# The residual of the last out-projection, scaled at other places of a hand-written order

## The chip, the cores and the metric

The kernel runs on one core of one Trainium2 chip. The metric is device time in microseconds (us), the median of 3 runs. One further execution was taken by the hardware profiler; all rows of the profile and the trace come from that one.

## What is computed

A decoder trunk of two layers on x of 512 rows (tokens) and 2048 columns, all in float32. Layer 0 is a differential attention, layer 1 a forgetting attention with 16 heads of 128 columns. Each layer ends alike:

```
y = o @ w_out                                  # out-projection, 2048 x 2048
x = layer_norm(DN_ALPHA * x + gate * y, ln_g[l], ln_b[l])
```

The change concerns layer 1. Its x is the normalised output of layer 0, x = n * g0 + b0, where the kernel keeps the plain n in DRAM and applies layer 0's weights g0, b0 (`ln_g[0]`, `ln_b[0]`) and the factor ALPHA only when the residual is needed. So the residual is ALPHA * (n * g0 + b0), and the row to be normalised is that plus gate * y.

## The kernel before

**Weights.** All products are made in three passes from two parts of each operand (`products`, L188 to L190: high x high, high x low, low x high). A `WeightStream` brings the weights of all jobs through four stage buffers (`wst`, L48, on the queue of SyncE, SP). ScalarE (ACT) rounds a stage to its high part `whi` (L108), VectorE (DVE) subtracts it to get the low part `wlo` (L109). `get` keeps this two slices ahead of the matmuls; there are three buffers of each part.

**The last out-projection** (`out_projection(oB, 1, ...)`) has four jobs, f = 0 to 3, of 512 output columns each. A job has eight slices of two 128-row weight tiles; for each slice `group` runs four bursts, one for each block b of 128 tokens, of six matmuls each. So a job has 32 bursts and 192 matmuls; each block accumulates in a PSUM bank of its own (`acc`, four in all), and job f + 1 needs the banks of job f back. In the last slice each block is evacuated by DVE: `ztmp` = acc * gate (L988), z = residual + ztmp (L1433), statistics (L990). In the last job, six of the slices are held back and run block by block, and the norm follows each block (`norm_b`).

**Pieces.** After each burst `tick` takes one entry off the list `pieces`: None, a function, or a list of functions. So other work is written between the bursts by hand. `last_pairs` puts the attention of heads 12 to 15 on that list in 50 steps (`score`, `turn`, `send`, `take`, `values`, and `og`, the split of a head's output, L184). The two half jobs ahead of the out-projection (16 bursts each) use 32 of them; 18 are left for job 0, and are steps 0 to 17 below:

```
[tc_[2]], [sd[2], tc_[3], og[8]], [rd[0], vc[0]], [vc[1], rd[1]], [sd[3], og[9]], [dd[0], dd[1], rd[2]], [og[10]],
[rd[3], dd[2]], [dd[3], og[11]], [td[0]], [td[1], og[12]], [td[2]], [td[3], og[13]], [vd[0]], [vd[1]], [], [og[14]], [og[15]],
```

Here c and d stand for heads 14 and 15. `score` is three matmuls into `sc`, the masked maximum on DVE (L1289), the exponential on ACT (L1292) and the normalisation; `turn` a transpose on DVE (L1303) and a store to DRAM (L1305); `send` four loads from there into `pTl` (L1313); `take` a cast to `pTh` on ACT (L1319) and a subtraction on DVE (L1320); `values` the matmuls into `o` and, in its second half, the head's output `ogB` on DVE (L1336).

**The residual.** `prepare(k)` calls `residual_b(f, banks)`: it issues the loads of g0, b0 (both broadcast over the partitions, L950) and of four blocks `nr` of n (L1415), and puts four functions `scaled(b)` on the list. Each is a pair on DVE, `nr = nr * ALPHA * g0` (L1419) and `nr = b0 * ALPHA + nr` (L1420), 512 columns wide. `prepare(0)` runs ahead of job 0, and looks for free (None) steps from the third on; there is one, step 15. So the four `scaled` of f = 0 stand at steps 15, 18, 19 and 20, `prepare(1)` at 21, and the `scaled` of f = 1 at 23, 25, 27 and 29. Only 28 steps can be taken ahead of job 0's first evacuation: there `drain()` runs all that is left. In job 1 `prepare(2)` stands behind eight free steps and its `scaled` at every second step after it (10, 12, 14, 16); job 2 is the same with `prepare(3)`.

**Who orders the instructions.** The order in which the code traces instructions is a priority, not the order in a queue. A planner at compile time fills each engine's queue: by its own estimates of durations and landings it takes, whenever an engine is free, the earliest traced instruction that is ready. Each engine then works through its queue in that fixed order. `tc.keep_in_program_order` (on L1419) ties an instruction behind the one that was traced last before it on the same engine; L1420 needs L1419's result. The loads have no such tie.

**Buffers.** The residual's tiles, `gate`, the heads' keys and outputs and some held weights share one pool of 16 buffers of 128 x 512 (`kpool`, tag "K"), which are given out in turn.

Of the kernel before, what the change touches and what calls it, by code (L numbers as in the profile page):

```python
# [124 lines left out]
def tile_yoco(  # L125
# [173 lines left out]
    pieces = []  # L299
# [571 lines left out]
    def drain():  # L871
        while pieces:
            tick(0)
# [71 lines left out]
    def ktile(name):  # L945
        return kpool.tile([P, T], F32, name=name, tag="K")


    def row_bcast(t, src):
        nc.sync.dma_start(t, src.partition_broadcast(P))  # L950
# [10 lines left out]
    def out_projection(jobs, layer, zp, opened, residual, norm, after_held=None):  # L961


        ready = {}

        def prepare(k):
            if k < len(jobs):
                ready[k] = residual(jobs[k][0], jobs[k][2])

        prepare(0)  # L970
        for k, (f, job, banks) in enumerate(jobs):
            if layer == 1:

                pieces.extend([None] * (8 if k else 0) + [lambda k=k: prepare(k + 1)])
            elif k:
                prepare(k)
            res = ready[k]
            gate = ktile("gate")
            row_bcast(gate, gate_dram[layer][0, 512 * f : 512 * (f + 1)])

            def evac(b, acc, f=f, res=res, gate=gate):
                if f == 0 and b == 0:
                    drain()
                    opened()
                pool, z, stats = zp
                zs = z[:, b, 512 * f : 512 * (f + 1)]
                tmp = pool.tile([P, 512], F32, name="ztmp", tag="htmp", bufs=2)
                V.tensor_tensor(tmp, acc, gate, op=ALU.mult)  # L988
                res(b, zs, tmp)
                V.bn_stats(stats[:, b, f, :], zs)  # L990
                if f == 3:
                    norm(b)

            last = k == len(jobs) - 1
            group(job, True, evac, banks, bg=1 if k == 0 and layer == 0 else 0, hold=(5, 6)[layer] if last else 0, after_held=after_held if last else None)
# [79 lines left out]
    pieces.append(lambda: split_og((14, 15)))  # L1075
    pieces.append(lambda: ab.update(kv=fold(0, ktile("mrow"))))
    out_projection(oA, 0, zp, open_n, residual_a, norm_a, lambda b, k: build_next() if b == 3 and k < 2 else None)
    npool, n, nstats = zp

# [320 lines left out]
    def open_z():  # L1400
# [3 lines left out]
        for k, src in (("g", ln_g), ("b", ln_b)):  # L1404
            lnrow[k] = pool.tile([P, D], F32, name="ln_" + k)
            row_bcast(lnrow[k], src[1, :])

    def residual_b(f, banks):
        fs = slice(512 * f, 512 * (f + 1))
        g0, b0 = ktile("g0"), ktile("b0")  # L1410
        row_bcast(g0, ln_g[0, fs])
        row_bcast(b0, ln_b[0, fs])
        nr = {b: ktile("nr") for b in banks}
        for b in banks:
            nc.sync.dma_start(nr[b], n_dram[b * P : (b + 1) * P, fs])  # L1415

        def scaled(b):

            tc.keep_in_program_order(V.scalar_tensor_tensor(nr[b], nr[b], ALPHA, g0, op0=ALU.mult, op1=ALU.mult))  # L1419
            V.scalar_tensor_tensor(nr[b], b0, ALPHA, nr[b], op0=ALU.mult, op1=ALU.add)  # L1420

        if f == 0:

            free = [k for k, piece in enumerate(pieces) if piece is None and k > 1]
            for k, b in zip(free, banks):
                pieces[k] = lambda b=b: scaled(b)
            pieces.extend(lambda b=b: scaled(b) for b in banks[len(free):])
        else:
            for b in banks:
                pieces.extend([None, lambda b=b: scaled(b)])  # L1430

        def fn(b, dst, tmp):
            V.tensor_tensor(dst, nr[b], tmp, op=ALU.add)  # L1433
        return fn

    def norm_b(b):
# [16 lines left out]
        for f0, f1 in zip((0, *ends), ends):  # L1453
            fs = slice(f0, f1)
            V.scalar_tensor_tensor(z[:, b, fs], z[:, b, fs], rstd, lnrow["b"][:, fs], op0=ALU.mult, op1=ALU.add)
            nc.sync.dma_start(out[b * P : (b + 1) * P, fs], z[:, b, fs])

    out_projection(oB, 1, zp2, open_z, residual_b, norm_b)
    drain()

# [27 lines left out]
```

## Time and profile before

| | us |
|---|---|
| median of 3 runs | 1970.49 (1969.86 to 1970.54) |
| the profiled execution | 1971.12 |
| its span, first to last instruction | 1969.3 |
| last out-projection: first matmul | 1769.30 |
| last statistics of its last block | 1958.61 |

A row of a timeline reads: start and length in us, engine, line of the kernel, operation, output <- inputs, shape, count, and in brackets the idle time before it and who ended it. PE is TensorE's matmul, PEld its weight load (which overlaps PE), DVE is VectorE, ACT ScalarE, SPq the queue of SyncE that issues the loads. A matmul's row is longer than the step from one matmul to the next, because they are pipelined. Rows named x2 hold two instructions.

### The profile page before, as it was taken

The numbers are of one execution on the slowest core, as the hardware profiler recorded it, in microseconds if no ns is written. First come the engines' busy times: TensorE is split into PE (matmuls) and PEld (weight loads), VectorE is DVE, ScalarE is ACT, GpSimd is POOL, SyncE is SP. The second block draws the span as 40 slices with busy tenths as digits, with TensorE's granted clock in tenths as the row PEclk, the third lists the DMA queues.
The fourth block names the chain that finished last, engine by engine and source line by source line (L and its number), as shares of the span: only waits on it lengthen the run. The fifth ranks groups of instructions, "written<-read, shape, count | busy, mean of one in ns | idle before, by whom it ended". The sixth has DMA issues, their size and how long they took to land.

```text
span 1969.3 us, 25096 instructions
## 1 busy us (share of the span) xinstructions
PE 1930.4 (98%) x8869; PEld 1600.0 (81%) x8869; DVE 1321.1 (67%) x2328; ACT 708.9 (36%) x1233; POOL 2.2 (0%) x10
## 2 busy tenths in 40 slices
PE   5999999999999999999999999999999999999997
PEld 4888888888888888888888888888888888887885
DVE  7885678877777777553575656566566666696557
ACT  2432445333333434431273222224343433452123
POOL 0000000000000000000000000000000000000000
PEclk8999999999999999999999999999999999999999
DMA  9993465777777775253336766664355555557432
GB/s 341 359 309 108 153 195 174 247 230 233 227 239 231 227 240 168 93 169 98 125 134 218 248 235 195 227 214 129 114 151 153 152 154 154 157 150 255 147 96 97
DMA packets 303002, 371.40 MB, mean 189 GB/s; under 512 B 57462, under 2 KB 221068, under 8 KB 302108
## 3 DMA queue, kind: packets, MB, share of 16 engines
q1 hardware_dynamic: 300496, 365.57, 58.4%
q10 hardware_dynamic: 2380, 4.21, 0.6%
q8 instruction: 70, 1.15, 0.2%
q14 instruction: 56, 0.46, 0.1%
HBM read 343.27 MB, written 26.43 MB: 188 GB/s over the span
## 4 chain that ended last, share of the span: by engine, by line
PE 94%; DVE 3%; DMA 1%; SPq 1%; issue 0%; ACT 0%; DVEq 0%; ACTq 0%
PE acc L188 28%; PE acc L189 28%; PE acc L190 28%; PE sc L189 2%; PE sc L190 2%; PE sc L188 2%; PE o L188 1%; PE o L190 1%; PE o L189 1%; DMA sms<-in_w_mod_dram 1%; SPq L497 1%; PE tr L847 0%; DVE wlo L109 0%; DMA wst<-in_b_w_out_dram 0%; PE sc L1046 0%
## 5 line engine op out<-in xcount | busy, mean ns | idle before, releaser
L109 DVE TENSOR_TENSOR wlo<-wst,whi 128x1024 fp32r<-128x1024 f32 (+2 forms) x322 | 384.0, 1194 | 374.1 <-ACT whi L108 362.2
L108 ACT CAST whi<-wst 128x1024 fp32r<-128x1024 f32 (+2 forms) x322 | 331.8, 1031 | 727.0 <-PE acc L190 354.3
L188 PE MATMUL acc<-whi,hh 128*128 128x512 f32 x1232 | 483.4, 395 | 4.6 <-DVE ztmp L988 4.2
L189 PE MATMUL acc<-wlo,hh 128*128 128x512 f32 x1232 | 481.3, 391 | 0.8 <-DVE wlo L109 0.8
L190 PE MATMUL acc<-whi,hl 128*128 128x512 f32 x1232 | 481.1, 391 | 0.0
L188 PE MATMUL acc<-hh,whi 128*128 128x512 f32 x1184 | 463.7, 392 | 0.0
L189 PE MATMUL acc<-hl,whi 128*128 128x512 f32 x1184 | 461.7, 390 | 0.0
L190 PE MATMUL acc<-hh,wlo 128*128 128x512 f32 x1184 | 461.4, 390 | 0.0
L188 PEld LDWEIGHTS acc<-whi,hh 128*128 128x128 f32 x1232 | 232.3, 189 | 51.5 <-DVE ztmp L988 4.7
L190 PEld LDWEIGHTS acc<-whi,hl 128*128 128x128 f32 x1232 | 231.9, 188 | 49.2
L189 PEld LDWEIGHTS acc<-wlo,hh 128*128 128x128 f32 x1232 | 232.3, 189 | 47.0 <-DVE wlo L109 1.1
L190 PEld LDWEIGHTS acc<-hh,wlo 128*128 128x128 f32 x1184 | 222.3, 188 | 47.3
L188 PEld LDWEIGHTS acc<-hh,whi 128*128 128x128 f32 x1184 | 222.5, 188 | 42.6
L189 PEld LDWEIGHTS acc<-hl,whi 128*128 128x128 f32 x1184 | 222.6, 188 | 42.0
L416 DVE SCALAR_TENSOR_TENSOR macc<-ms,cact,macc 128x1024 f32<-128x1024 f32 (+1 forms) x180 | 197.9, 1100 | 27.9 <-DMA ms<-in_w_mod_dram 13.4
L524 DVE SCALAR_TENSOR_TENSOR sacc<-sms,cact,sacc 128x512 f32<-128x512 f32 (+1 forms) x127 | 89.5, 705 | 4.9 <-DMA sms<-in_w_mod_dram 1.3
L751 ACT ACTIVATE e<-e,mn 128x128 f32<-128x128 f32 (+3 forms) x64 | 36.0, 563 | 101.4 <-DVE mn L747 97.9
L1292 ACT ACTIVATE eb<-eb,mnb 128x128 f32<-128x128 f32 (+1 forms) x64 | 36.1, 564 | 86.2 <-DVE mnb L1289 86.1
L747 DVE CUSTOM_DVE_ANT_0 e<-sc,bias 128x128 f32<-128x128 f32 (+3 forms) x64 | 31.1, 486 | 23.1 <-PE sc L190 20.3
L416 DVE SCALAR_TENSOR_TENSOR macc<-msk,cact,macc 128x512 f32<-128x512 f32 x60 | 45.0, 749 | 1.4
L1289 DVE CUSTOM_DVE_ANT_0 eb<-sc,biasb 128x128 f32<-128x128 f32 (+1 forms) x64 | 31.1, 486 | 17.7 <-PE sc L190 16.9
L849 ACT ACTIVATE ogT<-tr,subg 128x128 f32<-128x128 f32 x64 | 20.0, 363 | 51.3 <-PE tr L847 51.3
(261 smaller groups left out, 1756.2 us busy)
## 6 DMA issues: line engine op xcount, KB each, us to landing
wst<-in_a_w_in_dram SPq DMA_DIRECT2D x240, 256.0 KB, 3.9
ms<-in_w_mod_dram SPq DMA_DIRECT2D x64, 512.0 KB, 4.5
ms<-in_kv_w_mod_dram SPq DMA_DIRECT2D x64, 512.0 KB, 4.2
wst<-in_kv_w_dram SPq DMA_DIRECT2D x64, 512.0 KB, 3.7
sms<-in_w_mod_dram SPq DMA_DIRECT2D x56, 512.0 KB, 6.8
wst<-in_b_w_in_dram SPq DMA_DIRECT2D x112, 256.0 KB, 3.0
wst<-in_a_w_out_dram SPq DMA_DIRECT2D x32, 512.0 KB, 3.7
msk<-in_w_mod_dram SPq DMA_DIRECT2D x64, 256.0 KB, 5.5
```

The source lines that it names most:

```text
L108: self.nc.scalar.copy(hi[:, :, :w], st[:, :, :w])
L109: self.nc.vector.tensor_tensor(lo[:, :, :w], st[:, :, :w], hi[:, :, :w].bitcast(F32), op=ALU.subtract)
L188: PE.matmul(dst, lhs[0], rhs[0], start=start, stop=False)
L189: PE.matmul(dst, lhs[0], rhs[1], start=False, stop=False)
L190: PE.matmul(dst, lhs[1], rhs[0], start=False, stop=stop)
L416: ins = V.scalar_tensor_tensor(acc, w, cact[:, kt : kt + 1], acc, op0=ALU.mult, op1=ALU.add)
L524: V.scalar_tensor_tensor(acc, w, sc, acc, op0=ALU.mult, op1=ALU.add)
L747: V.tensor_tensor_reduce(out=e[:, :w], in0=sc[:, :w], in1=st["bias"][:, (3 - i) * P :], scale=-1.0, scalar=3.0e38, op0=ALU.add, op1=ALU.mi ...
L751: S.activation(e[:, :w], e[:, :w], AF.Exp, bias=mn, scale=-1.0, accum_out=rs)
L849: S.activation(ogT[2 * h + e][:, i * P : (i + 1) * P], pt[:, e * P : (e + 1) * P], AF.Copy, scale=subg[:, e : e + 1])
L1289: V.tensor_tensor_reduce(out=e[:, :w], in0=sc[:, :w], in1=bias[:, :w], scale=-1.0, scalar=3.0e38, op0=ALU.add, op1=ALU.min, accum_out=mn)
L1292: S.activation(e[:, :w], e[:, :w], AF.Exp, bias=mn, scale=-1.0, accum_out=rs)
```

## The change

The `scaled` functions get other places. Those of f = 0 are added to steps 4, 7, 11 and 13 of the list, behind what stands there. Those of f = 1 are not put on the list by `residual_b` but kept in `later`, and job 1 begins its list with them, at bursts 2, 5, 8 and 11 (from 0); `prepare(2)` follows at 12 instead of 8, with its `scaled` at 14, 16, 18 and 20. `prepare(1)` now is step 18 of job 0 instead of 21. Jobs 2 and 3 keep their lists.

```diff
         for k, (f, job, banks) in enumerate(jobs):
             if layer == 1:
 
-                pieces.extend([None] * (8 if k else 0) + [lambda k=k: prepare(k + 1)])
+                if k == 1:
+                    for piece in later:
+                        pieces.extend([None, None, piece])
+                pieces.extend([None] * (8 if k > 1 else 0) + [lambda k=k: prepare(k + 1)])
             elif k:
                 prepare(k)
...
+    later = []
+
     def residual_b(f, banks):
...
         if f == 0:
 
-            free = [k for k, piece in enumerate(pieces) if piece is None and k > 1]
-            for k, b in zip(free, banks):
-                pieces[k] = lambda b=b: scaled(b)
-            pieces.extend(lambda b=b: scaled(b) for b in banks[len(free):])
+            for k, b in zip((4, 7, 11, 13), banks):
+                pieces[k] = [*pieces[k], lambda b=b: scaled(b)]
+        elif f == 1:
+            later.extend(lambda b=b: scaled(b) for b in banks)
         else:
             for b in banks:
                 pieces.extend([None, lambda b=b: scaled(b)])
```

## The prediction

> **What bounds the kernel now.** I read the page first, then the list of waits of TensorE for the last projection, then the chain of waits and the timelines around the one wait found there.
>
> ```profile
> span 1969.3 us, 25096 instructions
> PE 1930.4 (98%) x8869; PEld 1600.0 (81%) x8869; DVE 1321.1 (67%) x2328; ACT 708.9 (36%) x1233; POOL 2.2 (0%) x10
> PE 94%; DVE 3%; DMA 1%; SPq 1%; issue 0%; ACT 0%; DVEq 0%; ACTq 0%
> ```
>
> TensorE (PE) is busy 98% of the span and is 94% of the chain, so a change to VectorE (DVE) steps pays only where TensorE waits for them. In the list of waits with TensorE alone, from 1769 to 1909 us (jobs 0, 1 and 2 of the last out-projection), there is one row:
>
> ```profile
> PE acc L188 <- DVE ztmp L988: 4.2, 1, 4.2
> ```
>
> Columns: who waits for whom, total, times, longest. It is the first matmul of job 1, which waits for the accumulator that `ztmp` (L988) of job 0's first row block must empty. The chain of waits shows what DVE did meanwhile (start, length, what):
>
> ```profile
> 1815.08 0.68 DVE nr L1420
> 1815.76 0.67 DVE nr L1419 x2
> ...
> 1816.88 1.29 DVE nr L1420 x2
> 1818.17 1.20 DVE nr L1419 x2
> 1819.37 0.60 DVE nr L1420
> 1819.98 0.60 DVE nr L1419
> 1820.58 1.20 DVE nr L1420 x2
> 1821.78 0.61 DVE ztmp L988
> 1822.44 0.80 PE acc L188
> ```
>
> Eleven instructions of `scaled` (six L1420, five L1419) run back to back from 1815.08 to 1821.78, and `ztmp` stands behind them: 6.70 us, 0.61 each. They are the rest of f = 0 (one L1420 of block 1, both of block 2) and all eight of f = 1. By the code the first L1419 of f = 0 is tied behind the DVE instruction traced before it, the output of the last attention head (L1336), and the others follow it; the four steps of f = 1 are forced out by `drain()` just ahead of job 0's evacuation.
>
> The timeline of TensorE and its busy time by stretch (length, busy and count of PE, PEld, DVE, ACT, POOL, granted clock, DMA share, GB/s) price that wait:
>
> ```profile
> 1817.82 0.39 PE L190 MATMUL acc<-whi,hl 128*128 128x512 f32 x1
> 1822.44 0.80 PE L188 MATMUL acc<-whi,hh 128*128 128x512 f32 x1 [4.23 <-DVE ztmp L988]
> ...
> 1827.17 0.40 PE L190 MATMUL acc<-whi,hl 128*128 128x512 f32 x1
> ...
> 1831.95 0.39 PE L190 MATMUL acc<-whi,hl 128*128 128x512 f32 x1
> ```
> ```profile
> 1818.20:1822.40 4.20, 0.01 (x1) 0.00 (x0) 4.20 (x8) 1.04 (x1) 0.00 (x0) 0.73 0.92 330
> 1822.40:1826.80 4.40, 4.36 (x10) 3.48 (x11) 4.40 (x8) 0.00 (x0) 0.00 (x0) 0.50 0.26 88
> 1927.20:1931.00 3.80, 3.80 (x17) 3.15 (x18) 0.48 (x1) 0.44 (x1) 0.00 (x0) 1.00 0.00 0
> ```
>
> From 1827.17 to 1831.95 lie 21 matmul steps, 0.2276 us each. The matmul after 1817.82 was due at 1818.05 and came at 1822.44: 4.39 us lost. Then the granted clock is 0.50: from 1822.44 to 1827.17 lie 11 steps in 4.73 us, where 11 x 0.2276 = 2.50 would do: another 2.23 us. The wait is worth **6.62 us**, half as much again as the list of waits says.
>
> **The change part by part.** It adds and removes no instruction: 16 pairs L1419/L1420 stay 16 pairs, and so do the loads. Only their places differ.
>
> *The four pairs of f = 1* go from the end of job 0 to bursts 2, 5, 8 and 11 of job 1, each tied behind the split of weights (`wlo`) traced before it, and those are traced behind the whole evacuation of job 0. Eight of the eleven instructions leave: 8 x 0.61 = 4.9 us. That alone would let `ztmp` start at 1815.08 + 3 x 0.61 = 1816.91; the chain has 0.66 us from its start to the matmul, so TensorE could go on at 1817.57, with 0.48 us to spare before 1818.05.
>
> *The four pairs of f = 0* go into bursts 4, 7, 11 and 13 of job 0. The other three of the eleven leave too, `ztmp` can start at 1815.08 behind the same `wlo`, and the margin grows to 1818.05 - (1815.08 + 0.66) = 2.31 us. The later row blocks follow:
>
> ```profile
> 1821.70 1.28 DVE L988 TENSOR_TENSOR ztmp<-acc,gate 128x512 f32<-128x512 f32 x2
> ...
> 1828.88 1.20 DVE L109 TENSOR_TENSOR wlo<-wst,whi 128x1024 fp32r<-128x1024 f32 x1
> ...
> 1836.86 1.22 DVE L109 TENSOR_TENSOR wlo<-wst,whi 128x1024 fp32r<-128x1024 f32 x1 [4.17 <-ACT whi L108]
> ```
>
> The evacuation takes 1821.70 to 1828.88, 7.2 us, 3.6 for two blocks (two `ztmp`, two sums, two statistics), so the fourth `ztmp` ends 3.6 + 2 x 0.61 = 4.8 us after the first starts, at 1819.9; TensorE wants that bank 18 matmuls after 1818.05, at 1822.1. The whole ends at 1822.3 and the next `wlo` at 1823.5; TensorE reaches those weights 48 matmuls into job 1, at 1829.0. After that DVE idles 4.2 us ahead of each `wlo` (last row), and a pair takes 1.2, so the four pairs cost nothing in job 1. Even all four ahead of that first `wlo` would take 4.9 of its 5.5 us.
>
> Where do the pairs of f = 0 land? DVE in job 0, and the loads on the queue of SyncE (SP) with their time to landing:
>
> ```profile
> 1763.61 0.68 DVE L184 TENSOR_TENSOR hl<-ogB,hh 128x512 fp32r<-128x512 f32 x1
> ...
> 1777.80 0.69 DVE L1289 CUSTOM_DVE_ANT_0 eb<-sc,biasb 128x512 f32<-128x512 f32 x1
> ...
> 1780.10 0.71 DVE L1303 STREAM_TRANSPOSE tb<-eb 128x512 f32<-128x512 f32 x1
> 1780.73 0.65 DVE L1320 TENSOR_TENSOR pTl<-pTl,pTh 128x512 fp32r<-128x512 f32 x1
> 1782.79 1.23 DVE L109 TENSOR_TENSOR wlo<-wst,whi 128x1024 fp32r<-128x1024 f32 x1 [1.40 <-ACT whi L108]
> ...
> 1790.20 1.23 DVE L109 TENSOR_TENSOR wlo<-wst,whi 128x1024 fp32r<-128x1024 f32 x1 [3.60 <-ACT whi L108]
> ...
> 1803.55 1.15 DVE L1320 TENSOR_TENSOR pTl<-pTl,pTh 128x384 fp32r<-128x384 f32 x2
> ```
> ```profile
> 1766.96 4.77 SPq L1313 DMA_DIRECT2D pTl<-turned  x8
> ...
> 1772.72 2.03 SPq L1415 DMA_DIRECT2D nr<-n_dram  x4
> ```
> ```profile
> DMA to landing us min/median/max: 6.3/6.5/6.6
> ```
>
> Block 0's pair is now tied behind the split L184 of head 9 (1763.61), block 1's behind the transpose at 1780.10, block 2's behind the L1320 at 1803.55, block 3's behind head 13's L184. Its operands land late: the first `nr` at 1772.72 + 6.5 = 1779.2. DVE is full until 1781.4; behind that it idles 1.4 and 3.6 us (rows 1782.79 and 1790.20). If the planner puts the three early pairs there (3 x 1.2 = 3.7 us), the idle time covers them. Without that cover they push `wlo`, whose weights TensorE reaches two slices (10.9 us) later, so nothing yet is lost. Block 2's pair delays the last split before head 15's values by 1.2 us; now both are done at 1804.7:
>
> ```profile
> 1782.37 0.19 PEld L189 LDWEIGHTS o<-pTl,vbh 128*128 128x128 f32 x1
> 1807.91 0.40 PE L188 MATMUL o<-pTh,vbh 128*128 128x512 f32 x1
> ```
>
> The values start at 1807.91, 3.2 us later, so 2.0 are left.
>
> *The loads.* `prepare(1)` moves from step 21 to 18, six issues that pass weight loads on SP; `prepare(2)` moves from burst 8 of job 1 to 12, its pairs from bursts 10 to 16 to bursts 14 to 20, the same two bursts behind their loads. Six issues hold SP about 3 us (the row of four `nr` takes 2.03). Weights have room for that: their casts wait for TensorE to free a buffer, 21 times, and never for a load between 1769 and 1909:
>
> ```profile
> ACT whi L108 <- PE acc L190: 86.5, 21, 11.0
> ```
>
> I take zero, with 0 to 1 us as bounds. Behind the removed wait nothing is late next: the evacuation, the weights and the banks have the margins above, and jobs 2 and 3 follow as they are.
>
> Sum: 1971.12 us is the profiled execution (1969.3 of span and 1.8 around it); less 6.6 it gives 1964.5. The median shown is 0.6 lower, 1970.49, so the forecast is **1963.9 us**.
>
> **The rivals.** *The early pairs hold up the attention (slower).* DVE works its queue in order. Were block 0's pair written directly behind its tie (over at 1764.3), DVE would stand until 1779.2, and 1.2 us more. All that follows would be 16.1 us late; the split at 1780.73 ends at 1781.4 and TensorE loads it at 1782.37, so 1.0 us is absorbed and TensorE loses 15.1, and 2.2 for each of one or two slow clocks. Against the 6.6 gained that is 10.7 to 12.9 us on the loss side: 1981 to 1983. The change breaks even when the pair heads DVE's queue at 1779.2 + 1.2 - 1.0 + 2.2 - 6.6 = 1775.0; earlier is a loss. For it: the tie permits it and DVE is not idle there. Against it: the planner issues by its own estimate of landings, and that estimate is late, not early:
>
> ```profile
> 1778.53 0.72 ACT L1292 ACTIVATE eb<-eb,mnb 128x512 f32<-128x512 f32 x1 [1.49 <-DVE mnb L1289]
> ...
> 1779.25 0.60 ACT L1319 CAST pTh<-pTl 128x512 fp32r<-128x512 f32 x1
> ```
>
> ScalarE (ACT) sat idle 1.49 us for the exponential, though the cast behind it stands earlier in the program. So the planner took the cast's data, sent by 1771.73, as not there yet; the loads of `nr` are queued behind those sends, and their pair must follow later still than the exponential's input at 1777.80. The Trainium skill, DMA: Bandwidth & Descriptors, Anatomy of one DMA, fits about 2.0 us plus bytes over 436 GB/s for one way of issuing, 2.6 us for 256 KB as an estimate from it. By that page the first `nr` would be there near 1775.3 and break-even would move to about 1771; the trace has 6.3 to 6.6 us and decides.
>
> *A part is given back.* A pair between 1777.80 and the split at 1780.73 makes DVE wait up to 1.4 us for the landing and work 1.2, with block 1's pair too 2.4: 1.2 to 3.8 us, less the 1.0 of slack, 0.2 to 2.8 on TensorE. The slow clock may follow: 4.2 us of waiting brought it, while the two waits at the start of job 3 did not (granted 1.00 from 1927.20, above):
>
> ```profile
> PE acc L189 <- DVE wlo L109: 0.8, 1, 0.8
> PE acc L188 <- ACT whi L108: 0.4, 1, 0.4
> ```
>
> With and without 2.2 us for the clock that makes 1964.1 to 1968.9. The Trainium skill, TensorE: Matmul & The Clock Gate, What's actually happening, says that the clock halves after an idle window of about 3.4 us; by that page the upper end would be 1966.7.
>
> *It does not take.* If pairs still stood ahead of `ztmp` when bank 0 is done, nothing would change. Four instructions suffice to use up the 2.31 us; only block 2's two are tied late, behind 1803.55, and that is 11 us ahead of 1815.08. Then 1970.5.
>
> **How the numbers follow.** Forecast 0.76, part given back 0.14, slower 0.06, no effect 0.04. The forecast's own range runs from 1966.1 (only the wait of 4.39 comes back) to 1962.7 (job 3's 1.2 us go too). With half of the second case the range 1962.7 to 1967.0 holds 0.83. A measurement here tells 0.2%, 3.9 us, from no change: below 1966.5 is faster. That is the forecast and half of the second case: 0.83 faster; the other half and the last: 0.11 the same; 0.06 slower.
>
> **What would show it.** Right: no wait of TensorE for `ztmp` at the start of job 1, the granted clock 1.00 through jobs 0 to 2, `ztmp` directly behind a `wlo` about 4 us earlier against the first matmul of job 1, four pairs among job 1's first three slices of weights, and the pairs of f = 0 in DVE's idle time behind the split at 1780.73. Wrong: a wait of TensorE for `pTl` or `sc` in job 0, an L1419 whose predecessor idles for a load of `nr`, or TensorE waiting for `wlo` early in job 1.

## The result, and the profile after

| | us |
|---|---|
| before, median of 9 runs | 1970.54 (1969.53 to 1972.77) |
| after, median of 9 runs | 1963.83 (1963.06 to 1965.51) |
| ratio, 95% interval | 0.9965, 0.9954 to 0.9975 |
| span of the profiled execution | 1969.3 before, 1963.0 after |

The kernel became 6.7 us faster; 1963.9 had been forecast. The page of the kernel after:

```profile
span 1963.0 us, 25096 instructions
PE 1929.5 (98%) x8869; PEld 1600.0 (82%) x8869; DVE 1321.6 (67%) x2328; ACT 708.9 (36%) x1233; POOL 2.2 (0%) x10
PE 95%; DVE 2%; SPq 1%; DMA 1%; ACT 0%; issue 0%; DVEq 0%; ACTq 0%
```

Every engine has the same number of instructions and, within 0.9 us, the same work; only the span is shorter. In the list of waits the row for `ztmp` is gone, as is job 3's short one for `whi`; TensorE waits for nothing from 1765 to 1910. The one row that is left of the last projection:

```profile
PE acc L189 <- DVE wlo L109: 0.8, 1, 0.8
```

Busy time by stretch of the kernel after (length, PE, PEld, DVE, ACT, POOL, granted clock, DMA share, GB/s), the first two jobs' meeting in the middle row:

```profile
1769.00:1818.00 49.00, 49.00 (x227) 41.03 (x226) 30.93 (x55) 15.87 (x27) 0.00 (x0) 1.00 0.72 236
1818.00:1822.40 4.40, 4.40 (x21) 3.66 (x20) 4.40 (x8) 1.05 (x1) 0.00 (x0) 1.00 0.46 167
1822.40:1862.00 39.60, 39.60 (x177) 32.78 (x176) 23.36 (x31) 7.38 (x7) 0.00 (x0) 1.00 0.60 189
```

PE is as long as each stretch and the clock is 1.00: before, TensorE stood for 4.2 us in the middle stretch, and behind that the clock was 0.50 from 1822.40 to 1826.80. How much did this stage itself gain? The first and the last matmul into `acc` of the last projection, in the timelines of TensorE before and after:

```profile
1769.30 0.40 PE L188 MATMUL acc<-whi,hh 128*128 128x512 f32 x1
...
1956.73 0.39 PE L190 MATMUL acc<-held,hl 128*128 128x512 f32 x1
```
```profile
1770.14 0.40 PE L188 MATMUL acc<-whi,hh 128*128 128x512 f32 x1
...
1950.36 0.39 PE L190 MATMUL acc<-held,hl 128*128 128x512 f32 x1
```

187.43 us became 180.22: 7.21 us less. The prediction's wait and clock are 6.62 of that, job 3's wait for `whi` 0.4, and 0.2 are unexplained. The execution after entered the projection 0.84 us later, ahead of any moved instruction, so that the end comes 6.4 earlier.

VectorE of the kernel after, in job 0 and around the first `ztmp`. The lines have moved: `scaled` is L1424 and L1425, `ztmp` L991, the split of `pTl` L1323:

```profile
1781.58 0.65 DVE L1323 TENSOR_TENSOR pTl<-pTl,pTh 128x512 fp32r<-128x512 f32 x1
1783.63 1.23 DVE L109 TENSOR_TENSOR wlo<-wst,whi 128x1024 fp32r<-128x1024 f32 x1 [1.40 <-ACT whi L108]
1784.77 0.69 DVE L1424 SCALAR_TENSOR_TENSOR nr<-nr,g 128x512 f32<-128x512 f32 x1
...
1787.78 1.29 DVE L1425 SCALAR_TENSOR_TENSOR nr<-b,nr 128x512 f32<-128x512 f32 x2
...
1791.04 1.23 DVE L109 TENSOR_TENSOR wlo<-wst,whi 128x1024 fp32r<-128x1024 f32 x1 [1.37 <-ACT whi L108]
...
1803.53 0.69 DVE L1424 SCALAR_TENSOR_TENSOR nr<-nr,g 128x512 f32<-128x512 f32 x1
...
1804.86 0.68 DVE L1323 TENSOR_TENSOR pTl<-pTl,pTh 128x512 fp32r<-128x512 f32 x1
...
1815.92 1.28 DVE L991 TENSOR_TENSOR ztmp<-acc,gate 128x512 f32<-128x512 f32 x2
...
1823.10 1.20 DVE L109 TENSOR_TENSOR wlo<-wst,whi 128x1024 fp32r<-128x1024 f32 x1
```

Three pairs stand between 1784.77 and 1789.0, behind the split at 1781.58. Between the two `wlo` around them VectorE was idle for 4.80 us before (0.51, 0.69 and 3.60); now it is 1.37. The fourth pair, block 2's, starts at 1803.53, just ahead of the last split. `ztmp` follows its `wlo` directly and starts at 1815.92; in the profile before it started at 1821.70.

### The profile page after: what moved, and what is told of

Same layout as the page of the kernel before. It is cut to its first block, busy times and chain, and to the rows that moved or that the text cites. A ratio compares the mean times of both kernels' runs of the same rounds, so it can differ in the third digit from the quotient of the medians.

```text
span 1963.0 us, 25096 instructions
## 1 busy us (share of the span) xinstructions
PE 1929.5 (98%) x8869; PEld 1600.0 (82%) x8869; DVE 1321.6 (67%) x2328; ACT 708.9 (36%) x1233; POOL 2.2 (0%) x10
## 4 chain that ended last, share of the span: by engine, by line
PE 95%; DVE 2%; SPq 1%; DMA 1%; ACT 0%; issue 0%; DVEq 0%; ACTq 0%
PE acc L188 28%; PE acc L189 28%; PE acc L190 28%; PE sc L188 2%; PE sc L189 2%; PE sc L190 2%; PE o L188 1%; PE o L190 1%; PE o L189 1%; DVE wlo L109 1%; SPq L497 0%; PE tr L847 0%; PE tr L565 0%; DMA wst<-in_a_w_in_dram 0%; DVE sacc L524 0%
```

## The experiments

"Median" is that of the timed runs; the ratio is to the kernel before on the same chip, whose medians there were 1970.44 to 1970.87.

**One half of the change alone.** *f = 1's pairs to job 1, f = 0's as before.*

```diff
-            for k, b in zip((4, 7, 11, 13), banks):
-                pieces[k] = [*pieces[k], lambda b=b: scaled(b)]
+            free = [k for k, piece in enumerate(pieces) if piece is None and k > 1]
+            for k, b in zip(free, banks):
+                pieces[k] = lambda b=b: scaled(b)
+            pieces.extend(lambda b=b: scaled(b) for b in banks[len(free):])
```

> Only the pairs of f = 1 move to job 1; those of f = 0 stay at steps 15, 18, 19 and 20. Theory (the whole gain is the wait of TensorE for the first ztmp at the start of job 1 and the slow clock behind it, and DVE instructions ahead of that ztmp eat a margin of 2.31 us at 0.61 us each): in this queue two instructions of f = 0 stand between the last wlo and the ztmp, 1.2 us of the 2.31, so no wait: about 1963.8 us, the same as the changed kernel. Rival (the pairs of f = 0 in the attention are worth something of their own): at least 1 us above the changed kernel.

Median 1964.09 us, ratio 0.9966 (0.9953 to 0.9978). TensorE waits for nothing in jobs 0 to 2. VectorE, ahead of the first `ztmp`:

```profile
1813.70 1.23 DVE L109 TENSOR_TENSOR wlo<-wst,whi 128x1024 fp32r<-128x1024 f32 x1 [0.19 <-ACT whi L108]
1814.84 0.69 DVE L1425 SCALAR_TENSOR_TENSOR nr<-b,nr 128x512 f32<-128x512 f32 x1
1815.44 0.68 DVE L1424 SCALAR_TENSOR_TENSOR nr<-nr,g 128x512 f32<-128x512 f32 x1
1816.05 0.68 DVE L991 TENSOR_TENSOR ztmp<-acc,gate 128x512 f32<-128x512 f32 x1
```

Two instructions of f = 0 are still ahead of it, and the margin takes them. The move of f = 1's four pairs is enough.

*f = 0's pairs to their new steps, f = 1's as before.*

```diff
-                if k == 1:
-                    for piece in later:
-                        pieces.extend([None, None, piece])
-                pieces.extend([None] * (8 if k > 1 else 0) + [lambda k=k: prepare(k + 1)])
+                pieces.extend([None] * (8 if k else 0) + [lambda k=k: prepare(k + 1)])
...
-        elif f == 1:
-            later.extend(lambda b=b: scaled(b) for b in banks)
```

> Only the pairs of f = 0 move to steps 4, 7, 11 and 13; those of f = 1 stay on job 0's list, and are forced out by the drain at the latest. The planner writes them behind the first two ztmp and ahead of the other two. Theory: job 1 begins without a wait, but its third row block waits for its bank: ztmp of block 2 ends 14 instructions of 0.61 us behind the start of the first, 8.5 us, where it is due 2.31 + 0.66 + 2 x 1.37 = 5.7 us behind it: a wait of about 2.8 us, and up to 2.2 more if the clock halves: 1966.6 to 1968.8. Rival (f = 0's ties alone held everything up, so moving them is enough): 1963.8. Rival (f = 0 has no part in it): 1970.5.

Median 1963.36 us, ratio 0.9963 (0.9950 to 0.9977): the expectation was wrong. VectorE did what it said, the third `ztmp` is 7.8 us behind the first; but TensorE did not wait, and its clock stayed at 1.00:

```profile
1815.43 1.28 DVE L988 TENSOR_TENSOR ztmp<-acc,gate 128x512 f32<-128x512 f32 x2
...
1823.24 0.68 DVE L988 TENSOR_TENSOR ztmp<-acc,gate 128x512 f32<-128x512 f32 x1
...
1825.03 0.68 DVE L988 TENSOR_TENSOR ztmp<-acc,gate 128x512 f32<-128x512 f32 x1
```
```profile
1818.00:1822.40 4.40, 4.40 (x21) 3.66 (x20) 4.40 (x8) 1.05 (x1) 0.00 (x0) 1.00 0.69 260
```

The two programs differ in the order of TensorE's products at the start of job 1 (bank of `acc`, and how many products in a row; this is from the programs as built, since the rows of the trace don't name the bank):

```
after:      0 x6, 1 x6, 2 x6, 3 x6, 0 x6, 1 x6, 2 x6, 3 x6
f = 0 only: 0 x6, 1 x6, 0 x6, 1 x6, 0 x1, 2 x8, 3 x6, 2 x4, 3 x6
```

The planner knew that banks 2 and 3 would be late and put the second slice's products into banks 0 and 1 ahead: 25 products, not 12, come before bank 2, 13 x 0.2276 = 3.0 us of work for a delay of 2.8. Is that order what hid the wait? The same kernel, with the second slice tied behind the last product of the first:

```diff
+                    with tc.issue_after(pinned[1]) if job is pinned[0] and s == 1 else ExitStack():
+                        end = products(acc[b][:, :w], (Hh[kt][:, bs], Hl[kt][:, bs]), (hi[kk][:, :w], lo[kk][:, :w]), start, stop)
+                    if s == 0:
+                        pinned[1] = end.ins
...
+            pinned[0] = job if layer == 1 and k == 1 else None
```

> As the run with f = 0's pairs alone, with TensorE's products of job 1's second slice tied behind the last product of its first, so that TensorE takes the four banks of the first slice one after the other. In that run the third ztmp started at 1823.24 (over at 1823.9), and TensorE would reach bank 2 twelve products of 0.2276 us behind bank 0, near 1821.1. Theory (the planner had put work of banks 0 and 1 ahead, and that alone hid the wait): TensorE now waits some 2.8 us for the third ztmp and some 0.3 for the fourth; with the clock at 1.00 the time is 1966.4, with the surplus that the runs with 7 and 9 added instructions had over their wait 1967.5. Rival (the instructions behind the first two ztmp cost nothing for another reason): no wait, 1963.4.

Median 1968.35 us (1966.91 to 1969.29), ratio 0.9986 (0.9977 to 0.9995). The banks now go 0, 1, 2, 3, VectorE's order around the four `ztmp` is the same as without the tie, and the wait is there; TensorE's timeline, then the busy time by stretch:

```profile
1823.64 0.50 PE L188 MATMUL acc<-whi,hh 128*128 128x512 f32 x1 [2.70 <-DVE ztmp L993]
...
1824.46 0.58 PE L188 MATMUL acc<-whi,hh 128*128 128x512 f32 x1
...
1828.10 0.39 PE L188 MATMUL acc<-whi,hh 128*128 128x512 f32 x1
```
```profile
1821.08:1824.49 3.41, 0.85 (x4) 0.70 (x5) 3.41 (x7) 0.00 (x0) 0.00 (x0) 1.00 0.03 11
1824.49:1827.90 3.41, 3.41 (x10) 2.58 (x9) 3.41 (x6) 0.00 (x0) 0.00 (x0) 0.50 0.00 0
1827.90:1831.30 3.40, 3.40 (x17) 2.81 (x16) 1.63 (x2) 1.05 (x1) 0.00 (x0) 1.00 0.48 159
```

So the order of the products hid 2.7 us of waiting; 2.8 had been expected, and of the 0.3 for the fourth `ztmp` nothing shows. The profiled execution lost more to the halved clock: from 1824.46 to 1828.10 lie nine steps in 3.64 us, where 9 x 0.2276 = 2.05 would do, another 1.6. Its span, 1966.7 us, is 4.0 above that of the untied kernel, 1962.7, and 2.7 + 1.6 are 4.3. The median lies above both values expected, 1966.4 and 1967.5, which had the clock at 1.00.

**A dose of work ahead of the first `ztmp`.** The kernel after, with n further instructions of `scaled`'s kind and size there, which compute nothing that is used; `ztmp` is tied behind them. For n = 11:

```diff
-                V.tensor_tensor(tmp, acc, gate, op=ALU.mult)
+                if layer == 1 and f == 0 and b == 0:
+                    for i in range(11):
+                        spare = z[:, i % 4, 512 * (1 + i // 4) : 512 * (2 + i // 4)]
+                        tc.keep_in_program_order(V.scalar_tensor_tensor(spare, gate, 1.0, gate, op0=ALU.mult, op1=ALU.mult))
+                    tc.keep_in_program_order(V.tensor_tensor(tmp, acc, gate, op=ALU.mult))
+                else:
+                    V.tensor_tensor(tmp, acc, gate, op=ALU.mult)
```

> The changed kernel with eleven DVE instructions of the same size as scaled (128 x 512, values not used) written directly ahead of the first ztmp of job 0. Theory: 11 x 0.61 = 6.7 us, less the margin of 2.31: TensorE waits 4.4 us and the clock halves for 2.2 more: 1970.4, as before the change. Rival (the gain came from the other places that moved with it, loads, weights or the attention, and not from the place ahead of ztmp): under 1967.

> The changed kernel with 5 further instructions of 0.61 us (3.05 us) on VectorE directly ahead of the first ztmp of job 1; they write parts of z that are overwritten later, and their values are unused. In the changed kernel that ztmp starts at 1815.92 and TensorE does not wait. Theory (margin of 2.31 us, then every further us is waited for): TensorE waits 3.05 - 2.31 = 0.7 us for ztmp, the granted clock stays 1.00, time 0.7 above the changed kernel: about 1964.5. Rival (the program is planned anew around a delay that it foresees, as in the runs with block 0's pair ahead and with f = 0's pairs alone): no wait, 1963.8.

> As the run with 5, with 7 instructions (4.27 us). Theory: TensorE waits 4.27 - 2.31 = 2.0 us for ztmp; if the clock needs a wait of some 3 us or more to be halved it stays at 1.00, and the time is 1965.8; if 2 us are enough, another 2.2 us go and it is 1968. Rival (planned anew): no wait, 1963.8.

> As the run with 5, with 9 instructions (5.49 us). Theory: TensorE waits 5.49 - 2.31 = 3.2 us for ztmp; with the clock at 1.00 the time is 1967.0, with the clock at 0.50 for some 4.7 us behind the wait, as after 4.2 us of waiting, it is 1969.2. Rival (planned anew): no wait, 1963.8.

> As the run with 9 added instructions, with 10 (6.07 us). The runs with 5, 7, 9 and 11 waited 0.6, 1.8, 3.0 and 4.2 us, each dose less 2.4: here 3.7 us. Clock: 1.00 behind 3.0 us and 0.50 for some 4.7 us behind 4.2 in the profiled executions. If the point lies at a fixed length between, this run falls on one side of it: 1967.5 with the clock at 1.00, 1969.7 with it halved. If it depends on more than the length, the timed executions spread over both.

> As the run with 10 added instructions, with 8 (4.86 us): a wait of 2.4 us, clock 1.00 behind it in the profiled execution, 1966.2. If part of the executions halve the clock behind such a wait too, as the timed executions of the run with 7 suggest (1964.2 to 1968.7), the median lies above that by up to 2 us and the mean granted clock of the higher ones is 0.994 in place of 0.995.

| n | added, us | TensorE's wait | added less wait | clock behind it | median (range) | ratio (interval) |
|---|---|---|---|---|---|---|
| 5 | 3.01 | 0.6 | 2.4 | 1.00 | 1965.47 (1964.11 to 1966.27) | 0.9969 (0.9957 to 0.9980) |
| 7 | 4.22 | 1.8 | 2.4 | 1.00 | 1967.13 (1964.24 to 1968.71) | 0.9979 (0.9970 to 0.9988) |
| 8 | 4.81 | 2.4 | 2.4 | 1.00 | 1967.90 (1966.56 to 1969.49) | 0.9986 (0.9977 to 0.9995) |
| 9 | 5.42 | 3.0 | 2.4 | 1.00 | 1968.45 (1966.70 to 1970.22) | 0.9988 (0.9979 to 0.9996) |
| 10 | 6.02 | 3.6 | 2.4 | 0.50 | 1970.33 (1967.84 to 1971.86) | 0.9997 (0.9988 to 1.0006) |
| 11 | 6.62 | 4.2 | 2.4 | 0.50 | 1970.49 (1968.92 to 1972.37) | 1.0000 (0.9991 to 1.0008) |

Waits and clocks are those of the profiled executions. "Added" is from the start of the first added instruction to that of `ztmp`. For n = 11, VectorE and the list of waits:

```profile
1817.58 6.70 DVE L994 SCALAR_TENSOR_TENSOR z<-gate 128x512 f32<-128x512 f32 x11
1824.20 0.68 DVE L995 TENSOR_TENSOR ztmp<-acc,gate 128x512 f32<-128x512 f32 x1
```
```profile
PE acc L188 <- DVE ztmp L995: 4.2, 1, 4.2
```

Eleven foreign instructions at that place give back the whole gain and the same wait as before, 4.2 us. Each dose less its wait is 2.4: that is the margin, forecast at 2.31. The rival of these runs, a new plan around the delay, is refuted for them: the waits are there. All four banks are late here, and that TensorE then has no other product to bring forward is the likely reason.

The waits came as expected within 0.2 us, the times did not. For n = 5, 7, 8, 9 and 10 the medians lie 1.0, 1.3, 1.7, 1.5 and 0.6 us above what was expected with the clock that the profiled execution then showed. Against 1964.2 (the kernel of the next part, timed beside n = 5, 7 and 9) those three lie 0.6, 1.1 and 1.2 us higher than their waits explain, even n = 5, whose profiled execution shows no lowered clock. A halved clock in some of the timed executions would be a cause, and it isn't shown. With n = 7 and 9 most of the dearer executions list a mean clock of 0.994 and most of the cheaper ones 0.995. With n = 8, the run whose expectation named this sign, the two lie mixed (0.994 at 1966.83 us, 0.995 at 1968.89), so that part of its expectation failed. The scatter elsewhere is larger than these surpluses: the part of the span outside the last projection's matmuls is 1780.9 us in the profiled execution of n = 7 and 1784.4 in that of n = 11. The surplus stays open.

**Pairs put earlier.** *Steps 0 to 3 for f = 0.*

```diff
-            for k, b in zip((4, 7, 11, 13), banks):
+            for k, b in zip((0, 1, 2, 3), banks):
```

> The changed kernel with the four pairs of f = 0 tied to steps 0, 1, 2 and 3 of job 0's first half in place of 4, 7, 11 and 13. Theory (the tie only bounds a pair from below, and the planner issues it where it takes the landing to be over, behind the split at 1781.6): all four pairs stand behind the first wlo of job 1's weights, TensorE does not wait, 1963.8. Rival (the tie decides the place): VectorE stands for the landing of nr before 1779 with a split behind it, TensorE loses over 10 us, 1974 or more.

Median 1964.24 us, ratio 0.9964 (0.9952 to 0.9977). The pairs start behind the split, as in the kernel after:

```profile
1780.51 0.65 DVE L1323 TENSOR_TENSOR pTl<-pTl,pTh 128x512 fp32r<-128x512 f32 x1
1782.56 1.23 DVE L109 TENSOR_TENSOR wlo<-wst,whi 128x1024 fp32r<-128x1024 f32 x1 [1.40 <-ACT whi L108]
1783.71 1.28 DVE L1424 SCALAR_TENSOR_TENSOR nr<-nr,g 128x512 f32<-128x512 f32 x2
```

The step in the list is only a lower bound for the place; where the planner takes the operands to be there decides.

*Block 0's pair forced ahead of what job 0 traces for VectorE.* This builds a milder form of the slower rival: the pair stands ahead of the rest of VectorE's work, but not directly behind its tie at 1764.3.

```diff
-            group(job, True, evac, banks, bg=1 if k == 0 and layer == 0 else 0, hold=(5, 6)[layer] if last else 0, after_held=after_held if last else None)
+            with tc.issue_after(lead[0]) if layer == 1 and k == 0 else ExitStack():
+              group(job, True, evac, banks, bg=1 if k == 0 and layer == 0 else 0, hold=(5, 6)[layer] if last else 0, after_held=after_held if last else None)
...
-            tc.keep_in_program_order(V.scalar_tensor_tensor(nr[b], nr[b], ALPHA, g0, op0=ALU.mult, op1=ALU.mult))
+            first = V.scalar_tensor_tensor(nr[b], nr[b], ALPHA, g0, op0=ALU.mult, op1=ALU.mult)
+            tc.keep_in_program_order(first)
+            lead.append(first.ins)
...
-            for k, b in zip((4, 7, 11, 13), banks):
+            scaled(0)
+            for k, b in zip((7, 11, 13), banks[1:]):
```

> The changed kernel with block 0's pair of f = 0 traced at the start of job 0 and every DVE instruction traced in job 0 tied behind its first half, so that it heads the queue before its load has landed. Rival of the prediction, taken to its end: DVE has run the rest by 1770.7 on the clock of the kernel before, then stands until nr lands at 1779.2, and is some 9 us late for all of job 0's attention; less 1.0 of slack TensorE loses 8 us and 2 to 4 for the clock: 1974 to 1976. If TensorE loses under 3 us (below 1967), the attention in job 0 has more slack than the split at 1780.73 showed, and the rival could never have decided.

Median 1963.32 us, ratio 0.9963 (0.9950 to 0.9977): the expectation was wrong by over 10 us. VectorE did stand, for 4.8 us where 8.5 had been expected:

```profile
1772.42 0.42 DVE L1324 TENSOR_TENSOR pTl<-pTl,pTh 128x256 fp32r<-128x256 f32 x1
1777.62 0.69 DVE L1426 SCALAR_TENSOR_TENSOR nr<-nr,g 128x512 f32<-128x512 f32 x1 [4.78 <-DMA nr<-n_dram]
...
1780.97 0.68 DVE L1324 TENSOR_TENSOR pTl<-pTl,pTh 128x512 fp32r<-128x512 f32 x1
...
1788.54 0.68 DVE L1293 CUSTOM_DVE_ANT_0 eb<-sc,biasb 128x512 f32<-128x512 f32 x1
```

But TensorE waited for nothing between 1765 and 1910. The planner laid the queue behind the standing differently. The two runs entered the projection at different times (first matmul 1768.82 here, 1770.14 in the kernel after), so places are counted from there. Head 14's two splits, which TensorE takes first, come close behind the pair: the second starts at 12.2 us, only 0.7 later than in the kernel after (11.4). Head 15's maximum of 512 columns, which TensorE needs last, goes from 8.5 to 19.7 us. On TensorE the first and the second product of head 14's values are 3.0 us apart, with twelve products into `acc` between them, where the kernel after has 0.7 us:

```profile
1781.42 0.40 PE L188 MATMUL o<-pTh,vbh 128*128 128x512 f32 x1
...
1784.41 0.40 PE L189 MATMUL o<-pTl,vbh 128*128 128x512 f32 x1
```

## Why the prediction was right, point by point

*The wait is worth 6.62 us.* Right. The profile after lacks both the wait and the halved clock, the stage is 7.21 us shorter, and eleven instructions put back cost 6.4 to 7.2 (1970.49 against 1963.32 to 1964.09 of the three kernels timed beside it). Its 2.23 us for the clock are those of one execution: with n = 11 the wait was the same 4.2 us, but the clock was halved for 3.41 us in place of 6.82, and the eight steps from 1824.94 to 1828.38 took 1.62 us more than 8 x 0.2276. So it is in part luck that the forecast met the median to 0.1 us.

*f = 1's pairs alone suffice.* Right, as the first experiment shows; three instructions of f = 0 were expected ahead of `ztmp`, and two stood there. The reading that all pairs of f = 0 follow the last head's output (L1336) is not exact: one of them, block 3's by the code, already stood at 1802.22 in the kernel before, ahead of L1336 at 1810.53. The count of eleven instructions is right all the same.

*The margin with both moves, 2.31 us.* The list of waits gives 2.4. Counted as in the prediction, from the time at which the matmul was due, each wait is 0.16 us longer and the margin 2.23. The difference of 0.08 is in the 0.66 us from the start of `ztmp` to the matmul: the chain shows that start at 1821.78, the timeline at 1821.70, which makes 0.74.

*The evacuation takes 7.2 us, then f = 1's pairs are free.* Right: 1815.92 to 1823.10; the four pairs start at 1824.23, 1826.80, 1832.20 and 1833.53, and TensorE is full throughout job 1.

*f = 0's early pairs land in idle time behind the split.* Right in its effect. Three of them all stand behind the first of the two gaps named: the 1.40 us ahead of the `wlo` at 1783.63 are still idle, and the idle time behind it is what they use. The next `wlo` is 0.84 us later than before, 1791.04 against 1790.20, which is just the offset with which the projection began. Block 2's pair came where it was expected, and no wait followed.

*The loads cost nothing.* No wait for a load shows on TensorE in jobs 0 to 2, and the 7.21 us gained in the stage show no loss of 1 us beside the 6.62.

*The slower rival, 1981 to 1983.* It did not come, and the last experiment shows that its price was wrong, not only its chance. There the pair headed VectorE's queue from 1772.84, ahead of the 1775.0 at which the change was to break even. By the prediction's own sum, 4.8 us of standing and 1.2 of work less 1.0 of slack, TensorE should have lost 5.0 us; it lost nothing. The step that failed is "all that follows would be 16.1 us late": it took VectorE's queue behind the pair, and TensorE's, as they stood in the trace. Both are ordered anew for each kernel, and in that run head 14's splits went first while work that was needed later made room. The rival in full, 14.9 us of standing behind 1764.3, was not built, so what it would cost stays open. In that run the landing too was earlier than taken: the four `nr` were issued from 1771.75 on, and VectorE worked at 1777.62, at most 5.9 us later, where 6.5 stood in the sum; in the profile after the sixteen loads of `nr` landed in 4.2 to 6.2. The 2.6 us estimated in the prediction from the Trainium skill, DMA: Bandwidth & Descriptors, Anatomy of one DMA, are further off than that; that section gives its fit for DMAs issued from GpSimd, and these are issued from SyncE.

*The signs.* They came, but for one that the rows don't bear out: "`ztmp` about 4 us earlier against the first matmul of job 1". It starts 2.97 us ahead of that matmul (1815.92, 1818.89), where it was 0.74 ahead before (1821.70, 1822.44): 2.2 us earlier, because before the change the matmul itself was late.

*What the forecast owed to its shape.* The same reasoning holds for the wait that was removed: it existed because the planner had left all four banks behind the eleven instructions, and with them, it seems, nothing else for TensorE to do. With two banks free in time, as in the run with f = 0's pairs alone, the wait is gone without the other half of the change. Each half alone is worth the whole gain, and no version tried is measurably faster than the changed kernel (medians of 1963.3 to 1964.2 for the four that don't wait, ratios of 0.9963 to 0.9966 beside its 0.9965).

## What to carry to other kernels

A short wait of TensorE can cost more than its row in the list: read the granted clock behind it too. In the kernel before it added half as much again; behind the waits of n = 5 to 9 the profiled executions show a clock of 1.00. To remove it, ask what else that engine could do at the time: freeing two of four accumulator banks was as good as freeing all, because the planner filled the gap with their next products. And where a planner orders the queues, price a delay by the slack of the work that can be put behind it, not by shifting the traced queue; in two runs here such a delay was hidden whole (2.7 and 4.8 us), and where all four banks were late it was paid in full beyond the margin.

## What the runs showed of the clock

The length of a wait does not decide whether the clock is halved: 3.0 us left it at 1.00 (n = 9), 2.7 halved it (banks tied). The n = 9 and n = 10 kernels, and the kernel before, by stretches:

```profile
1817.10:1820.51 3.41, 1.51 (x7) 0.93 (x5) 3.41 (x7) 1.05 (x1) 0.00 (x0) 1.00 0.98 355
1820.51:1823.93 3.42, 2.29 (x10) 1.88 (x11) 3.42 (x7) 0.00 (x0) 0.00 (x0) 1.00 0.39 144
1823.93:1827.34 3.41, 3.41 (x17) 2.81 (x16) 3.41 (x7) 0.00 (x0) 0.00 (x0) 1.00 0.00 0
```
```profile
1818.50:1821.90 3.40, 1.24 (x6) 0.70 (x4) 3.40 (x6) 1.04 (x1) 0.00 (x0) 1.00 1.00 360
1821.92:1828.74 6.82, 5.37 (x13) 4.22 (x14) 6.82 (x13) 0.00 (x0) 0.00 (x0) 0.50 0.27 97
1828.74:1832.00 3.26, 3.26 (x16) 2.67 (x15) 2.88 (x4) 0.29 (x1) 0.00 (x0) 1.00 0.00 0
```
```profile
1816.77:1820.18 3.41, 1.44 (x7) 0.86 (x5) 3.41 (x7) 1.04 (x1) 0.00 (x0) 1.00 0.92 309
1820.18:1823.59 3.41, 1.15 (x3) 0.96 (x4) 3.41 (x7) 0.00 (x0) 0.00 (x0) 0.50 0.90 318
1823.59:1827.00 3.41, 3.41 (x10) 2.64 (x9) 3.41 (x6) 0.00 (x0) 0.00 (x0) 0.50 0.06 21
1827.00:1830.40 3.40, 3.40 (x17) 2.79 (x16) 3.09 (x5) 0.02 (x1) 0.00 (x0) 1.00 0.00 0
```

The halved stretches are 3.41 us long (banks tied, above; n = 11, from 1824.79) or 6.82, twice that, and they begin inside the wait (before, n = 10, n = 11) or 0.85 us after TensorE has restarted (banks tied: restart at 1823.64, halved from 1824.49). In the 3.41 us ahead of them TensorE was busy for 1.44 us (before), 1.24 (n = 10), 0.00 (n = 11) and 0.85 (banks tied).

Behind this lies a fixed grid, and each trace shows it: all times at which the granted clock changed are whole numbers of steps of 3.4133 us apart. From the first fall on, they are 28.18, 38.42, 1820.17, 1827.00 and 1960.12 us in the kernel before, with 3, 522, 2 and 39 steps between them; with n = 9 they are 28.52, 38.76 and 1957.05 us, with 3 and 562 steps. A wait that falls into one window counts in full there, and one that crosses a border is split. So it was with n = 9: the border at 1820.51 splits its 3.0 us, TensorE was busy for 1.51 us in one window and 2.29 in the next, and the clock stayed at 1.00. With n = 7 and 8 the emptiest windows held 1.73 and 1.83 us of work, and it stayed too. In the last projection, then, what TensorE did in a single window sorts the eight profiled executions with a wait: up to 1.44 us of work and the clock was halved behind it, 1.51 us or more and it was not. The way back needed more: the clock was 1.00 again behind a window with 3.27 us of work (n = 11), and not behind one with 1.96 (n = 10, 1821.92 to 1825.33).

These are no general bounds. At the start of the program, where TensorE does smaller products, the kernel after shows 2.91 us of busy TensorE from 27.91 to 31.31 and a clock of 0.50 behind it. The Trainium skill, TensorE: Matmul & The Clock Gate, What's actually happening, describes such a free-running window of 3413 ns, and the lengths here agree. It has the clock fall after an idle window; here windows with up to 1.44 us of work were followed by the halved clock. Where the grid lay in the timed executions isn't known, so the share of executions that pay stays open.
